# Turned-over attention rows kept in SBUF, attention operands on the other side of SBUF, token groups of 5, 6 and 5 blocks

## The chip, the cores and the metric

The kernel runs on one core of a Trainium2 chip. The metric is the device time of one launch in microseconds (us). The engines are PE (TensorE, matrix products), DVE (VectorE), ACT (ScalarE), POOL (GpSimd) and SP (SyncE, which here only issues transfers). Each engine executes its instructions in a fixed order; POOL and SP also issue DMA transfers, in that same order.

## The reference, cut to what matters

One layer of a hybrid decoder for a prompt of 2048 tokens and 8 single new tokens. A projection feeds two head groups: sparse attention (an indexer scores all earlier keys, the 256 best are kept, softmax over them) and a gated linear recurrence. Both outputs are joined, projected by `w_out` and added to x; a squared-ReLU MLP follows.

```python
h = rms_norm(x, norm1_g)
aq, ak, av, iq, ik, iw, rq, rf, ri, rg = jnp.split(h @ w_in, IN_OFFSETS, axis=-1)
...
att = attend(aq, ak, av, iq, ik, iw)             # top 256 keys by the indexer's scores, softmax over them
rec, S_new = hgrn2_mixer(rq, rf, ri, rg, lb, rec_norm_g, s0)
x = x + jnp.concatenate([att, rec.astype(att.dtype)], axis=-1) @ w_out
h2 = rms_norm(x, norm2_g)
x = x + jnp.square(jax.nn.relu(h2 @ w_up)) @ w_down
```

Widths: D = 1024, attention 512, recurrence 512, MLP 4096. The 8 new tokens attend to a paged cache of 16384 tokens each ("the sample"). All is float32.

## The kernel before, in words

The prompt is cut into 16 blocks of 128 tokens; block 16 stands for the 8 new tokens. Float32 accuracy is made of rounded parts: an operand is split into a high and a low part (`hh`/`hl`, `wh`/`wl`), and `mm3` (lines 126 to 129) runs three products.

`trunk` first does the projection, the recurrence and the indexer's scores for all blocks, and the choice of keys for blocks 2 to 7 (`early`, pool `px`). From about 1060 us on it goes through three groups of blocks, 0 to 5, 6 to 11 and 12 to 16:

- `attend` (function `attend_all`): for each block and each of 4 pairs of heads, logits `lg` against the keys `KS`, mask `MB` added on DVE, exponential on ACT, transposes `pt`, products with the values `VS` into `O`, back-transposes `ob`, and a scaling on POOL into the tile `att`. The finished `att` is stored to DRAM (`attD`, line 1028 and the lines after it). Keys, values and queries are loaded by DMAs on POOL's queue (`prep`, lines 939 to 960).
- `mlp` (function `mlp_group`): reads `attD` back as `mix` (`load_mix`), turns it over on PE (`transposed`, 4 transposes a block into `tp`) and splits it into `hh`, `hl`; projects by `w_out` (`po`, in four quarters `cq`); normalizes (`hn`, turned over into `hh`, `hl` again); then 16 panels of 256 hidden columns, each `up` (hidden values, in two token halves), ReLU and square on ACT (`rl`, `uh`), low part on DVE (`ul`, line 1705), and `dn` (products with `w_down`), which DVE adds to `y` (line 1729). Weights come in pieces of 512 KB: `raw` on SP's queue, a rounding copy on ACT (line 1550), and the low part from POOL (a subtraction at line 1554 in the first group, which stores it; from then on a DMA on POOL's queue at line 1552).

`recurrence_out` (recurrence rows times the lower half of `w_out`, `po<-wh,th`, kept in `yD`) is given to the scheduler beside the first group's attention. Two side tracks run along the first two MLPs: the choice of keys for blocks 8 to 11 and 12 to 15 (`Track` of `choose_all`, ACT and DVE), and the sample's parts (`part`): first the indexer's scores over the cache (indirect gathers `kg` on POOL, DVE transposes `kt`, splits `kh`, `kl`, products `sc`), then the search `tot`, a list of chosen rows, and 32 indirect gathers `KG`, `VG` on POOL (line 1473). A `Track` advances one step for every `rate` columns of matrix products (`PACE`, `PUMP`) that the MLP has put into the program; `issue_after` holds its instructions behind those last entered in the dictionary `front`.

The order on every engine is made at build time by a scheduler that simulates the program, with priorities (`high_priority`; a smaller one for stores, `LATE`). SBUF is given out by pools, from the left (low addresses) or the right; a tile in a place used before waits for the earlier tile's last use. Bytes of a partition: before, `p3` (with `hh`, `hl`, `y`) lies at 63424 to 152704, the attention's `pt` at 63424 upward and its `pk` with `KS`, `VS` at 123392 to 190976; `px` lies at 194528 to 224580.

Of the kernel before, what the change touches and what calls it, by code (L numbers as in the profile page):

```python
# [45 lines left out]
def hymba_kernel(ctx, tc, x_prompt, x_sample, cache_k, cache_v, cache_kidx, state_hgrn, page_table,  # L46
# [28 lines left out]
    def rows(t):  # L75
        return P if t < NB else NS
# [68 lines left out]
    GB = NB // NG  # L145


    GROUPS = range(6), range(6, 12), range(12, NB + 1)

    def trunk(ctx):  # L150

# [42 lines left out]
        def attend(tiles, LB, PT, OB):  # L194

            blocks = [b for b in tiles if b < NB]
            with tc.tile_pool(name="pt", bufs=1, reuse_waits="tile") as pt_, \
                 tc.tile_pool(name="pk", bufs=1, reuse_waits="tile") as pk, \
                 tc.tile_pool(name="qt", bufs=1, space=PSUM, reuse_waits="tile") as qt:
                yield from attend_all(pk, blocks)(pt_, qt, LB, PT, OB)  # L200

        def mlp(tiles):

            with tc.tile_pool(name="p3", bufs=1, reuse_waits="tile") as p3, \
                 tc.tile_pool(name="q3", bufs=1, space=PSUM, reuse_waits="tile") as q3:
                yield from mlp_group(tiles, p3, pw, q3, loads, E_IO, 2, 3, 4)
# [16 lines left out]
        choice = Track(choose_all(choose_block, range(AHEAD, GROUPS[2][0])), PACE[0])
        first = Track(part(), PUMP[0])
        with tc.tile_pool(name="pf", bufs=1, reuse_waits="tile") as pf, \
             tc.tile_pool(name="qf", bufs=1, space=PSUM, reuse_waits="tile") as qf:
            along(high(attend(GROUPS[0], 4, 2, 2), NEAR))
            recurrence_out(pf, qf)
        along(mlp(GROUPS[0]), choice, first)
        first.finish()  # L230
        choice.finish()
        choice = Track(choose_all(choose_block, GROUPS[2]), PACE[1])
        along(attend(GROUPS[1], 4, 4, 2))
        second = Track(part(), PUMP[1])
        along(mlp(GROUPS[1]), choice, second)
        second.finish()
        choice.finish()
# [661 lines left out]
    def recurrence_out(pf, qf):  # L899

        wh = pf.tile([P, 4, D], F32R, name="wh")
        wl = pf.tile([P, 4, D], F32R, name="wl")
        for k in range(4):
            raw = pf.tile([P, D], F32, tag="raw", name="raw", bufs=1)
            nc.sync.dma_start(raw, w_out[0, 512 + k * P:512 + (k + 1) * P])
            nc.scalar.copy(wh[:, k], raw)
            nc.gpsimd.tensor_tensor(wl[:, k], raw, wh[:, k].bitcast(F32), op=OP.subtract)
        for t in range(EARLY):
            rt = pf.tile([P, 512], F32, tag="rt", name="rt", bufs=2)
            nc.sync.dma_start(rt, recD[t * P:(t + 1) * P])  # L910
            y = pf.tile([P, D], F32, tag="y", name="y", bufs=2)
            nc.sync.dma_start(y, xp[t * P:(t + 1) * P])
            ps = qf.tile([P, 512], F32, tag="tp", name="tp", bufs=1)
            for k in range(4):
                nc.tensor.transpose(ps[:, k * P:(k + 1) * P], rt[:, k * P:(k + 1) * P], ident)
            th = pf.tile([P, 4, P], F32R, tag="th", name="th", bufs=2)
            tl = pf.tile([P, 4, P], F32R, tag="tl", name="tl", bufs=2)
            pv = ps.rearrange("p (k n) -> p k n", k=4)
            nc.scalar.copy(th, pv)
            nc.vector.tensor_tensor(tl, pv, th.bitcast(F32), op=OP.subtract)  # L920
            for hf in range(2):
                s = slice(hf * 512, (hf + 1) * 512)
                po = qf.tile([P, 512], F32, tag="po", name="po", bufs=1)
# [6 lines left out]
    def attend_all(pk, blocks):  # L930

        LEN = (blocks[-1] + 1) * P
        NC = (blocks[-1] + 4) // 4
# [98 lines left out]
        def attention(p2, q2, LB, PTB, OB):  # L1032
# [8 lines left out]
            for i, (b, u) in enumerate(units):  # L1041
# [542 lines left out]
    def w_out_parts(tiles):  # L1584
        return 1 if tiles[-1] < EARLY else 2

    def mlp_group(tiles, p3, pw, q3, loads, IO, MM, DN, UB):


        T = sum(rows(t) for t in tiles)  # L1590
# [5 lines left out]
        load_cols, load_row, load_mix = loads  # L1596

        def transposed(x, n, hi, lo, parts=2):

            for hf in range(parts):  # L1600
                ps = q3.tile([P, 512], F32, tag="dn", name="tp", bufs=DN)
                for k in range(4):
                    nc.tensor.transpose(ps[:, k * n:(k + 1) * n], x[:, (hf * 4 + k) * P:(hf * 4 + k + 1) * P], ident[:n, :n])
                pv = ps[:, :4 * n].rearrange("p (k n) -> p k n", k=4)
                hv = hi[:, hf * 4:hf * 4 + 4]
                nc.scalar.copy(hv, pv)
                nc.vector.tensor_tensor(lo[:, hf * 4:hf * 4 + 4], pv, hv.bitcast(F32), op=OP.subtract)

        hh = p3.tile([P, 8, T], F32R, tag="hh", name="hh")
        hl = p3.tile([P, 8, T], F32R, tag="hl", name="hl")  # L1610
# [162 lines left out]
```

## Time and profile before

| | us |
|---|---|
| median of 3 runs (3577.22 to 3578.02) | 3577.35 |
| the profiled execution | 3582.42 |
| its span, first to last instruction | 3580.7 |
| PE busy in the span | 3321.7 |
| DVE busy | 2341.7 |
| ACT busy | 2212.5 |
| mean granted PE clock, share of full speed | 0.965 |

The three groups lie so on the time axis: attention 0 from 1081 to 1291, MLP 0 to 1999, attention 1 from 2012, MLP 1 from about 2211 to 2903, attention 2 from 2912, MLP 2 from about 3122 to the end. In rows of waits, what stands behind "<-" is what was waited for.

### The profile page before, as it was taken

The page shows a single profiled execution, that of the slowest core. Times are in us where ns is not written, and L with a number is a line of the kernel's source. Part 1 is how long each engine was busy: PE and PEld are TensorE (multiplying, and loading weights), DVE is VectorE, ACT ScalarE, POOL GpSimd, SP SyncE. Part 2 cuts the span into 40 slices and gives each one's busy share as a digit, 9 for nine tenths or more (in the row PEclk, how much of TensorE's full clock was granted, in tenths as well). Part 3 has the DMA queues.
Part 4 walks back from the last instruction along what each step waited for, and adds up shares of the span by engine and source line. Part 5 has one row for each costly group of instructions (what it writes and reads, how often), then busy time and mean ns, then how long its engine had stood idle before and what let it go on. Part 6 is the DMA issues. An engine that isn't in the chain of part 4 may idle for free. (4 is left out here: it accounts for less than half of the span.)

```text
span 3580.7 us, 56788 instructions
## 1 busy us (share of the span) xinstructions
PE 3321.7 (93%) x20230; PEld 2911.3 (81%) x20230; DVE 2341.7 (65%) x5150; ACT 2212.5 (62%) x4063; POOL 1198.9 (33%) x1463
## 2 busy tenths in 40 slices
PE   8999989999998989999999898999699979889999
PEld 7786878999986778888888686889598868778888
DVE  3576798877773356898895588779636648633223
ACT  5789887767764347859843477476597337543332
POOL 5566676555552034544543110003400110021110
PEclk9999999999998999999999998899899989989999
DMA  7555556365534444555554411323443441155554
GB/s 213 161 171 162 155 162 181 112 165 142 156 109 164 137 163 145 186 164 155 168 190 141 156 46 50 113 95 107 144 127 109 153 163 36 42 186 168 177 169 143
DMA packets 347277, 509.13 MB, mean 142 GB/s; under 512 B 39048, under 2 KB 252016, under 8 KB 345840
## 3 DMA queue, kind: packets, MB, share of 16 engines
q1 hardware_dynamic: 284960, 333.96, 29.4%
q0 software_dynamic: 62032, 171.54, 15.9%
q8 instruction: 159, 2.61, 0.3%
q14 instruction: 126, 1.03, 0.1%
HBM read 379.25 MB, written 126.15 MB: 141 GB/s over the span
## 5 line engine op out<-in xcount | busy, mean ns | idle before, releaser
L509 ACT ACTIVATE jkA<-S,candA 128x1152 int8<-128x1152 f32 (+11 forms) x448 | 586.0, 1310 | 83.2 <-DVE candA L513 67.7
L1729 DVE TENSOR_TENSOR y<-y,dn 128x512 f32<-128x512 f32 x512 | 346.7, 682 | 304.6 <-PE dn L129 302.5
L127 PE MATMUL up<-hh,wh 128*128 128x384 f32 (+2 forms) x1536 | 493.3, 321 | 10.9 <-ACT wh L1550 5.7
L128 PE MATMUL up<-hl,wh 128*128 128x384 f32 (+2 forms) x1536 | 491.6, 320 | 0.0
L129 PE MATMUL up<-hh,wl 128*128 128x384 f32 (+2 forms) x1536 | 487.8, 321 | 3.1 <-DMA wl<-low 1.6
L128 PE MATMUL dn<-dl,uh 128*128 128x512 f32 x1024 | 405.8, 396 | 29.4 <-DMA dl<-low 29.4
L127 PE MATMUL dn<-dh,uh 128*128 128x512 f32 x1024 | 403.2, 397 | 2.1 <-DVE y L1729 1.5
L129 PE MATMUL dn<-dh,ul 128*128 128x512 f32 x1024 | 400.7, 394 | 0.0
L127 PEld LDWEIGHTS up<-hh,wh 128*128 128x128 f32 x1536 | 292.0, 190 | 22.9 <-ACT wh L1550 7.4
L128 PEld LDWEIGHTS up<-hl,wh 128*128 128x128 f32 x1536 | 292.2, 190 | 13.8 <-issue 4.2
L129 PEld LDWEIGHTS up<-hh,wl 128*128 128x128 f32 x1536 | 290.4, 190 | 12.5 <-POOL wl L1554 2.7
L1705 DVE TENSOR_TENSOR ul<-rl,uh 128x384 fp32r<-128x384 f32 (+1 forms) x192 | 117.2, 611 | 199.0 <-ACT uh L1704 197.7
L128 PEld LDWEIGHTS dn<-dl,uh 128*128 128x128 f32 x1024 | 193.5, 189 | 61.5 <-DMA dl<-low 30.2
L974 PE MATMUL lg<-KS,aqT 128*128 128x512 f32 (+3 forms) x640 | 199.8, 411 | 45.4 <-DMA KS<-ksD 34.2
L1550 ACT CAST dh<-raw 128x1024 fp32r<-128x1024 f32 x96 | 97.0, 1046 | 231.1 <-PE dn L129 223.3
L129 PEld LDWEIGHTS dn<-dh,ul 128*128 128x128 f32 x1024 | 193.2, 189 | 43.4
L983 ACT ACTIVATE L<-L,nm 128x128 f32<-128x128 f32 (+15 forms) x128 | 154.2, 1205 | 119.6 <-DVE nm L982 118.7
L127 PEld LDWEIGHTS dn<-dh,uh 128*128 128x128 f32 x1024 | 193.4, 189 | 39.6 <-DVE y L1729 3.8
L487 DVE SCALAR_TENSOR_TENSOR sl<-ix,iw,sl 128x512 f32<-128x512 f32 (+3 forms) x266 | 180.1, 677 | 59.1 <-ACT ix L483 56.6
L481 PE MATMUL ix<-IK,iqT 128*128 128x512 f32 (+3 forms) x608 | 187.9, 394 | 31.1 <-DVE sl L487 20.7
L483 ACT ACTIVATE ix<-ix,iw 128x512 f32<-128x512 f32 (+3 forms) x304 | 182.2, 603 | 50.8 <-PE ix L481 50.2
L1702 ACT ACTIVATE rl<-up 128x384 f32<-128x384 f32 (+1 forms) x192 | 86.8, 452 | 194.8 <-PE up L129 192.3
(497 smaller groups left out, 9270.5 us busy)
## 6 DMA issues: line engine op xcount, KB each, us to landing
raw<-in_w_up_dram SPq DMA_DIRECT2D x96, 512.0 KB
raw<-in_w_down_dram SPq DMA_DIRECT2D x96, 512.0 KB
wl<-low POOLq DMA_DIRECT2D x72, 512.0 KB
raw<-in_w_in_dram SPq DMA_DIRECT2D x256, 128.0 KB
dl<-low POOLq DMA_DIRECT2D x64, 512.0 KB
wl<-lowp POOLq DMA_DIRECT2D x48, 512.0 KB
low<-wl SPq DMA_DIRECT2D x40, 512.0 KB
low<-dl SPq DMA_DIRECT2D x32, 512.0 KB
```

The source lines that it names most:

```text
L127: nc.tensor.matmul(ps, lh, rh, start=first, stop=False)
L128: nc.tensor.matmul(ps, lh, rl, start=False, stop=False)
L129: nc.tensor.matmul(ps, ll, rh, start=False, stop=last)
L481: nc.tensor.matmul(ps[:, :kn], iqT[:, h], IK[:, i, k0:k0 + kn], start=i == 0, stop=i == 1)
L483: nc.scalar.activation(r[:, :kn], ps[:, :kn], AF.Relu, scale=iw[:, 1, h:h + 1])
L487: nc.vector.scalar_tensor_tensor(sl, r[:, :kn], iw[:, 2, h:h + 1], sl, op0=OP.mult, op1=OP.add)
L509: nc.scalar.activation(jk[:, :n], S[:, :n], AF.Sign, bias=cand.bitcast(F32), scale=-1.0, accum_out=cnt)
L974: nc.tensor.matmul(ps[:, :kn], aqT[:, 2 * u + j], KS[k0 // 512][:, u // 2, i, :kn], start=i == 0, stop=i == 1)
L983: nc.scalar.activation(L[:, :n], L[:, :n], AF.Exp, bias=nm, scale=ATT_SCALE, accum_out=sm[:, j:j + 1])
L1550: nc.scalar.copy(wh, raw)
L1705: nc.vector.tensor_tensor(ul[:, o], rl[:, :cn], uh[:, o].bitcast(F32), op=OP.subtract)
L1729: front["dve"] = nc.vector.tensor_tensor(ys_[t][:, s], ys_[t][:, s], po, op=OP.add)
```

## The change

1. **Turned-over rows.** A pool `ph` holds `hh` and `hl` of a group from before its attention until its MLP is done (`group_rows`). When a block's attention is finished, `turned` transposes `att` straight into it. `attD` and `mix` are used only for the 8 new tokens.
2. **Sides.** `pk` (keys, values, now also `aqT` and `MB`) is opened on the right side; `px` is closed before each attention and opened again after it (`choosing`). Bytes of a partition after: `ph` 63424 to 112576, `p3` and `pt` from 104384 (groups 0 and 2) or 112576 (group 1) upward, `pk` 163808 to 229344. `pk` then shares places with `px` and the sample's pools, and `pt` with `p3`'s `y`.
3. **Groups** of 5, 6 and 5 blocks (and the 8 new tokens). The choice still takes blocks 8 to 11 in MLP 0 and 12 to 15 in MLP 1.
4. **Smaller edits.** `front["pool"]` makes the tracks' instructions stand behind the last weight piece that POOL handled; `PUMP` 8000 becomes 7000 in MLP 0; `O` has one buffer in attention 0 (2 before), `L` 4 in attention 2 (5 before); `recurrence_out` has one `y` and two `po` buffers (2 and 1 before).

```diff
-    GROUPS = range(6), range(6, 12), range(12, NB + 1)
+    GROUPS = range(5), range(5, 11), range(11, NB + 1)
...
+        def group_rows(tiles):
+            T = sum(rows(t) for t in tiles)
+            ph = ctx_.enter_context(tc.tile_pool(name="ph", bufs=1, reuse_waits="tile"))
+            return [ph.tile([P, 8, T], F32R, name=x) for x in ("hh", "hl")]
...
-            with tc.tile_pool(name="pt", bufs=1, reuse_waits="tile") as pt_, \
-                 tc.tile_pool(name="pk", bufs=1, reuse_waits="tile") as pk, \
+            with tc.tile_pool(name="pk", bufs=1, side="right", reuse_waits="tile") as pk, \
+                 tc.tile_pool(name="pt", bufs=1, reuse_waits="tile") as pt_, \
...
+        with ExitStack() as ctx_:
+            rows_ = group_rows(GROUPS[1])
+            along(attend(GROUPS[1], rows_, 4, 4, 2))
+            choice = choosing(range(LATER, NB), PACE[1])
+            second = Track(part(), PUMP[1])
+            along(mlp(GROUPS[1], rows_), choice, second)
+            second.finish()
+            choice.finish()
+            cx.close()
...
-    PACE, PUMP = (12000, 14000), (8000, 9000)
+    PACE, PUMP = (12000, 14000), (7000, 9000)
...
-            aqT = p2.tile([P, NH, P], F32R, tag="aqT", name="aqT", bufs=2)
+            aqT = pk.tile([P, NH, P], F32R, tag="aqT", name="aqT", bufs=2)
...
                 if u == 3:
-                    (nc.gpsimd if b == blocks[-1] else nc.sync).dma_start(attD[b * P:(b + 1) * P], att)
+                    c = (b - blocks[0]) * P
+                    turned(q2, "pt", PTB, att, P, *(x[:, :, c:c + P] for x in rows_), 1)
...
-                nc.gpsimd.dma_start(wl, lowD[key])
+                front["pool"] = nc.gpsimd.dma_start(wl, lowD[key])
             else:
-                nc.gpsimd.tensor_tensor(wl, raw, wh.bitcast(F32), op=OP.subtract)
+                front["pool"] = nc.gpsimd.tensor_tensor(wl, raw, wh.bitcast(F32), op=OP.subtract)
...
-            if t < NB:
-                transposed(mx_[:n], n, hh[:, :, c:c + n], hl[:, :, c:c + n], 1 if t < EARLY else 2)
-            else:
-                transposed(mx_[:n], n, st[:, :, :NS], st[:, :, 32:])
+            if t == NB:
+                transposed(load_mix(t)[:n], n, st[:, :, :NS], st[:, :, 32:])
```

`turned` is the body of the former `transposed` with the PSUM pool and tag as arguments.

The instruction lists of PE, DVE and ACT hold the same operations with the same shapes in the same numbers before and after (the 64 block transposes read `att` instead of `mix`); what differs is their order, and that 16 stores to `attD` and 16 loads from it are gone. The order shows three places. The first is POOL in MLP 1, where the sample's row gathers `KG`, `VG` stand among the weight pieces `wl`, `dl` (`low`: a stored low part). Before:

```order
L1552 DMA wl<-low_19288 128x1024
L1552 DMA wl<-low_19296 128x1024
L1442 TENSOR_TENSOR ol<-o_28793,keyb 128x44x8
L1473 DMA KG<-in_cache_k_dram,idx 128x128 x16
L1473 DMA VG<-in_cache_v_dram,idx 128x128 x16
L1552 DMA dl<-low_19531 128x1024
L1552 DMA dl<-low_19539 128x1024
```

And now:

```order
L1572 DMA wl<-low_18649 128x1024
L1572 DMA wl<-low_18657 128x1024
L1462 TENSOR_TENSOR ol<-o_27908,keyb 128x44x8
L1493 DMA KG<-in_cache_k_dram,idx 128x128 x2
L1572 DMA dl<-low_18877 128x1024
L1572 DMA dl<-low_18885 128x1024
L1493 DMA KG<-in_cache_k_dram,idx 128x128 x4
L1572 DMA wl<-low_19055 128x1024
L1572 DMA wl<-low_19063 128x1024
L1493 DMA KG<-in_cache_k_dram,idx 128x128 x4
```

The next panel's `dl` stood behind all 32 gathers; it now stands behind two of them. The second place is POOL at the end of MLP 1, where the loads of attention 2 (`aqT`, `KS`, `VS`) stand. Before:

```order
L1552 DMA dl<-low_22892 128x1024
L1552 DMA dl<-low_22900 128x1024
L1552 DMA wl<-low_15776 128x1024
L1554 TENSOR_TENSOR wl<-raw,wh 128x1024
L1552 DMA wl<-low_15852 128x1024
L942 DMA aqT<-qsD 128x1024
L946 DMA KS_32390<-ksD 128x2048
L947 DMA VS_32394<-vsD 128x1024
```

And now:

```order
L1572 DMA wl<-low_21846 128x1024
L1572 DMA wl<-low_21854 128x1024
L961 DMA aqT<-qsD 128x1024
L965 DMA KS_31511<-ksD 128x2048
L966 DMA VS_31515<-vsD 128x1024
...
L966 DMA VS_31518<-vsD 128x1024
L1572 DMA dl<-low_21990 128x1024
L1572 DMA dl<-low_21998 128x1024
L1572 DMA wl<-low_22086 128x1024
L1572 DMA wl<-low_22094 128x1024
L1572 DMA dl<-low_22230 128x1024
L1572 DMA dl<-low_22238 128x1024
```

They stood behind the MLP's last weight piece (`low_22900`) and three pieces of the next `w_out`; they now stand ahead of the last two `dl` pairs and the last `wl` pair. DVE's last mask of the choice, which frees their place, stands ahead of the last 33 of the MLP's 192 additions to `y` (36 before). In the same way attention 1's loads now stand ahead of the last `dl` pair of MLP 0. The third place is PE between attention 2 and MLP 2. Before:

```order
L1013 MATMUL O<-pl,VS_32397 128x256
L1020 MATMUL ob<-ident,ot 128x128 x2
L1603 MATMUL tp<-ident,mix 128x128 x12
L127 MATMUL po<-wh,hh 128x256
L128 MATMUL po<-wl,hh 128x256
```

And now:

```order
L1032 MATMUL O<-pl,VS_31518 128x256
L1039 MATMUL ob<-ident,ot 128x128 x2
L1612 MATMUL tp<-ident,att 128x128 x4
L1612 MATMUL tp<-ident,mix 128x8 x8
L127 MATMUL po<-wh,hh 128x256
L128 MATMUL po<-wl,hh 128x256
L129 MATMUL po<-wh,hl 128x256
```

Only the last block's four transposes and the new tokens' eight are left between the attention and `w_out`; the others stand within the attention. At the start of attention 0 its first logits now stand among the last head's recurrence products (`lv`), and at its end the last three pairs of heads stand without products of `recurrence_out` between them.

## Rows read from the trace of the kernel before

**Rows 1.** The page's first part: engine, busy us, share of the span, instructions.

```profile
PE 3321.7 (93%) x20230; PEld 2911.3 (81%) x20230; DVE 2341.7 (65%) x5150; ACT 2212.5 (62%) x4063; POOL 1198.9 (33%) x1463
```

**Rows 2.** Busy time by stretch: length, engines, PE clock, DMA share, GB/s.

```profile
1060.00:1140.00 80.00, 62.47 (x277) 43.70 (x276) 26.98 (x109) 34.42 (x95) 32.99 (x40) 0.81 0.52 178
1280.00:1400.00 120.00, 95.96 (x589) 86.53 (x589) 68.01 (x154) 70.52 (x119) 47.17 (x52) 0.90 0.53 172
1400.00:1910.00 510.00, 491.79 (x2452) 436.06 (x2451) 448.53 (x863) 370.72 (x625) 238.98 (x162) 0.99 0.53 167
1995.00:2040.00 45.00, 29.47 (x148) 21.94 (x147) 22.63 (x68) 15.80 (x34) 7.63 (x15) 0.81 0.60 217
2195.00:2320.00 125.00, 101.63 (x639) 93.60 (x639) 97.08 (x232) 70.32 (x107) 11.70 (x25) 0.84 0.35 112
2540.00:2600.00 60.00, 26.78 (x125) 23.35 (x124) 26.90 (x75) 38.01 (x42) 30.13 (x30) 0.72 0.41 133
2895.00:2945.00 50.00, 29.89 (x144) 22.35 (x143) 22.39 (x63) 12.06 (x18) 6.71 (x13) 0.76 0.59 218
3100.00:3200.00 100.00, 80.84 (x569) 74.75 (x567) 38.34 (x70) 42.55 (x73) 20.14 (x32) 0.88 0.51 162
3200.00:3580.00 380.00, 376.16 (x2317) 326.48 (x2314) 114.61 (x190) 130.69 (x238) 41.19 (x118) 1.00 0.49 164
```

**Rows 3.** PE's waits, 2540 to 2600: who for whom, us, times, longest.

```profile
PE dn L128 <- DMA dl<-low: 28.3, 1, 28.3
```

**Rows 4.** POOL in order of time, 2480 to 2640: start, us, line, operation, idle before.

```profile
2529.68 1.10 POOL L1473 DMA_INDIRECT KG<-in_cache_k_dram,idx  x1 [20.05 <-DVE idx L1462]
...
2575.48 1.21 POOL L1552 DMA_DIRECT2D dl<-low  x2
...
2603.86 0.53 POOL L1552 DMA_DIRECT2D dl<-low  x1 [26.12 <-PE dn L129]
...
2636.29 0.53 POOL L1552 DMA_DIRECT2D dl<-low  x1 [20.21 <-PE dn L129]
```

**Rows 5.** PE's waits at the two switches from an MLP to an attention.

```profile
PE lg L974 <- DMA KS<-ksD: 15.0, 2, 12.5
PE lg L974 <- DMA KS<-ksD: 19.2, 4, 9.4
```

**Rows 6.** Chain that ended last, 2895 to 2945: start, us, what.

```profile
2907.01 18.50 DMA KS<-ksD
```

**Rows 7.** PE's waits from an attention to its MLP: 1280 to 1400, 2195 to 2320, 3100 to 3200.

```profile
PE po L127 <- ACT hh L1606: 6.7, 1, 6.7
PE tp L1603 <- DVE hn L1661: 5.3, 4, 2.2
...
PE tot L1317 <- DVE jk L1313: 8.3, 3, 5.1
...
PE tp L1603 <- DMA mix<-attD: 4.2, 2, 3.1
PE po L128 <- DMA wl<-low: 3.0, 1, 3.0
```

**Rows 8.** Two stretches of MLP 0, columns as in rows 2.

```profile
1560.00:1600.00 40.00, 33.68 (x164) 29.59 (x163) 38.43 (x66) 20.59 (x37) 17.06 (x10) 0.96 0.56 175
1800.00:1840.00 40.00, 35.84 (x171) 30.59 (x170) 39.87 (x61) 17.42 (x32) 19.61 (x15) 0.96 0.56 186
```

**Rows 9.** DVE's groups, 1400 to 1910: line, operation, count, busy us, mean ns.

```profile
L1729 DVE TENSOR_TENSOR y<-y,dn 128x512 f32<-128x512 f32 x150 | 99.7, 676 | 11.1 <-PE dn L129 10.6
L1705 DVE TENSOR_TENSOR ul<-rl,uh 128x384 fp32r<-128x384 f32 x50 | 39.1, 782 | 4.8 <-ACT uh L1704 3.7 <-ACT rl L1703 0.8
```

**Rows 10.** Waits of POOL and of PE, 1400 to 1910.

```profile
POOL kg L1249 <- DVE kt L1251: 176.6, 43, 13.5
...
PE up L129 <- POOL wl L1554: 0.8, 1, 0.8
```

**Rows 11.** DMA between 2895 and 2935: packets, bytes, mean rate.

```profile
DMA packets 2452, 10.88 MB, mean 272 GB/s; under 512 B 273, under 2 KB 273, under 8 KB 1938
```

More of the change, by code (lines that the diff above doesn't have):

```diff
@@ L192, in trunk, with attend, mlp @@
         loads = mlp_loads(pw, E_IO, E_WB)
[L194 removed]
+        def group_rows(tiles):
+            T = sum(rows(t) for t in tiles)
+            ph = ctx_.enter_context(tc.tile_pool(name="ph", bufs=1, reuse_waits="tile"))
+            return [ph.tile([P, 8, T], F32R, name=x) for x in ("hh", "hl")]
+        def attend(tiles, rows_, LB, PT, OB):
             blocks = [b for b in tiles if b < NB]
[L197 to L198 removed]
+            with tc.tile_pool(name="pk", bufs=1, side="right", reuse_waits="tile") as pk, \
+                 tc.tile_pool(name="pt", bufs=1, reuse_waits="tile") as pt_, \
                  tc.tile_pool(name="qt", bufs=1, space=PSUM, reuse_waits="tile") as qt:
[L200 to L202 removed]
+                yield from attend_all(pk, blocks, rows_)(pt_, qt, LB, PT, OB)
+        def mlp(tiles, rows_):
             with tc.tile_pool(name="p3", bufs=1, reuse_waits="tile") as p3, \
                  tc.tile_pool(name="q3", bufs=1, space=PSUM, reuse_waits="tile") as q3:
[L206 removed]
+                yield from mlp_group(tiles, p3, pw, q3, loads, rows_, E_IO, 2, 3, 4)
         def part():
@@ L221, in along, with choosing @@
                         t.step()
[L223 to L237, printed above, removed]
-        cx.close()
+        cx.close()
+        def choosing(blocks, rate):
+            px = cx.enter_context(tc.tile_pool(name="px", bufs=1, side="right", reuse_waits="tile"))
+            return Track(choose_all(choose_keys(px), blocks), rate)
+        with ExitStack() as ctx_:
+            rows_ = group_rows(GROUPS[0])
+            with tc.tile_pool(name="pf", bufs=1, reuse_waits="tile") as pf, \
+                 tc.tile_pool(name="qf", bufs=1, space=PSUM, reuse_waits="tile") as qf:
+                along(high(attend(GROUPS[0], rows_, 4, 2, 1), NEAR))
+                recurrence_out(pf, qf)
+            choice = choosing(range(AHEAD, LATER), PACE[0])
+            first = Track(part(), PUMP[0])
+            along(mlp(GROUPS[0], rows_), choice, first)
+            first.finish()
+            choice.finish()
+            cx.close()
+        with ExitStack() as ctx_:
+            rows_ = group_rows(GROUPS[1])
[4 more added lines that the diff above has]
+            second.finish()
+            choice.finish()
+            cx.close()
         for _ in picks:
             pass
-        along(attend(GROUPS[2], 5, 4, 2))
-        along(mlp(GROUPS[2]))
+        with ExitStack() as ctx_:
+            rows_ = group_rows(GROUPS[2])
+            along(attend(GROUPS[2], rows_, 4, 4, 2))
+            along(mlp(GROUPS[2], rows_))
     def high(steps, offset):
@@ L286, in choose_all @@
             yield "choice"
-    PACE, PUMP = (12000, 14000), (8000, 9000)
-    AHEAD = 8
+    PACE, PUMP = (12000, 14000), (7000, 9000)
+    LATER = 12
     NEAR = 100000
@@ L910, in recurrence_out @@
             nc.sync.dma_start(rt, recD[t * P:(t + 1) * P])
-            y = pf.tile([P, D], F32, tag="y", name="y", bufs=2)
+            y = pf.tile([P, D], F32, tag="y", name="y", bufs=1)
             nc.sync.dma_start(y, xp[t * P:(t + 1) * P])
@@ L922, in recurrence_out @@
                 s = slice(hf * 512, (hf + 1) * 512)
-                po = qf.tile([P, 512], F32, tag="po", name="po", bufs=1)
+                po = qf.tile([P, 512], F32, tag="po", name="po", bufs=2)
                 for k in range(4):
@@ L927, in recurrence_out, with attend_all @@
             store(yD[t], y)
-    def attend_all(pk, blocks):
+    def attend_all(pk, blocks, rows_):
         LEN = (blocks[-1] + 1) * P
@@ L952, in prep @@
             n = (b + 1) * P
-            MB = p2.tile([P, cols], BF, tag="MB", name="MB", bufs=2)
+            MB = pk.tile([P, cols], BF, tag="MB", name="MB", bufs=2)
             if n > TOPK:
@@ L1585, in w_out_parts, with turned, mlp_group @@
         return 1 if tiles[-1] < EARLY else 2
-    def mlp_group(tiles, p3, pw, q3, loads, IO, MM, DN, UB):
+    def turned(pool, tag, bufs, x, n, hi, lo, parts):
+        for hf in range(parts):
+            ps = pool.tile([P, 512], F32, tag=tag, name="tp", bufs=bufs)
+            for k in range(4):
+                nc.tensor.transpose(ps[:, k * n:(k + 1) * n], x[:, (hf * 4 + k) * P:(hf * 4 + k + 1) * P], ident[:n, :n])
+            pv = ps[:, :4 * n].rearrange("p (k n) -> p k n", k=4)
+            hv = hi[:, hf * 4:hf * 4 + 4]
+            nc.scalar.copy(hv, pv)
+            nc.vector.tensor_tensor(lo[:, hf * 4:hf * 4 + 4], pv, hv.bitcast(F32), op=OP.subtract)
+    def mlp_group(tiles, p3, pw, q3, loads, rows_, IO, MM, DN, UB):
         T = sum(rows(t) for t in tiles)
@@ L1598, in transposed @@
         def transposed(x, n, hi, lo, parts=2):
[L1600 to L1610, printed above, removed]
+            turned(q3, "dn", DN, x, n, hi, lo, parts)
+        hh, hl = rows_
         ys_ = {}
```

1 line of the change is left out of this document (removed).

## The prediction

> **What bounds the kernel now.** I read the page's first part, then the waits of PE, then busy time by stretch, then the order of time on POOL at the worst stretch. PE is busy 3321.7 of 3580.7 us, no other engine above 65% [rows 1], so PE is the bound as a whole and 259 us of PE idle time are all that a change of order can win, plus what the lower of the two clock levels (1.2 instead of 2.4 GHz) costs. The reader is to see in the stretches that the idle time isn't spread evenly: MLP 2 has 376 busy us in 380 at clock 1.00, MLP 0 492 in 510, but the seams between stages are poor, and each seam also shows a lower mean clock, 0.72 to 0.90 [rows 2]. The clock falls where PE stood idle before, and PE's next work then runs at the lower level.
>
> The instruction lists of PE, DVE and ACT are the same before and after, with the same shapes, so no term comes from more or less computing. Groups of 5, 6, 5 have token halves of 384 and 256, 384 and 384, 384 and 264 columns where 6, 6, 4 had twice 384 and 384, then 256 and 264: the same six. What a group loses another gains. The sum below is therefore one of idle time and clock, stretch by stretch. Idle is the stretch's length less PE's busy time; the clock costs at most (1 - clock) times busy, and less where the low clock fell into the idle time itself.
>
> **The change part by part.**
>
> *The gather stall (2540 to 2600).* Idle 33.2 us, clock at most 0.28 x 26.8 = 7.5 [rows 2]. PE waits once for 28.3 us for `dl` [rows 3]. On POOL the first gather waits 20 us for `idx`, 32 gathers follow until 2575.5, and only then comes `dl` [rows 4]. With two gathers ahead of it, `dl` would be issued about 2.5 us after 2529.7, or when its buffer is free, so before 2551, where PE began to wait. The rest of the gathers follow between later pieces. They finish some panels later (a panel of MLP 1 takes 2636.3 - 2603.9 = 32.4 us, rows 4), with their reader still panels away. I take 31; bounds 0 (the wait for `idx` still blocks the queue until too late) and 40.
>
> *From an MLP to the next attention (1995 to 2040, 2895 to 2945).* Idle 15.5 and 20.1, clock at most 5.6 and 7.2 [rows 2]; PE waits 15.0 and 19.2 for `KS` [rows 5], and in the chain of waits `KS` alone ends 18.5 us [rows 6]. The cause is the place: `KS` lay on `p3`'s uses, so loading began when the MLP ended. On the right side it waits for the choice and the sample, which end 33 additions, 33/12 = 2.75 panels or 89 us before MLP 1's end, and some 1.6 panels before MLP 0's. What is late next: `L` now lies on `y`, so the first logits wait for stores of `y`. In attention 2 the first `L` lies on `hl` and the first `y` tile, long free; in attention 1 on the third and fourth `y` of five, stored a few us behind the end. I take 11 and 20, bounds 5 to 18 and 12 to 25.
>
> *The loads' new place in POOL's queue.* They now stand ahead of the last two `dl` pairs. The attention's loads of some 7 MB moved at 272 GB/s as a mean [rows 11], so about 26 us. Of the 33 additions behind the choice 24 belong to the last two panels and 9 to the one before, so the loads are issued 9 additions of 1.35 us (16.2 us of `dn` over 12), 12 us, before that panel's end frees the next `dl` buffers; that `dl` is needed half a panel (16 us) later: 28 us against 26. I take a loss of 2, bounds 0 and 25. The Trainium skill speaks against this place: its page "DMA: Bandwidth & Descriptors", section "Queues, rings and completion order", says that a DMA engine consumes the descriptors of one ring in order, so weights issued behind the loads on one queue are served behind them. By that rule alone the `dl` pair comes after all 7 MB, which is the rival "loads ahead of weights" below; no row of before shows weights queued behind such loads.
>
> *From an attention to its MLP (1280 to 1400, 2195 to 2320, 3100 to 3200).* Idle 24.0, 23.4, 19.2; clock at most 9.6, 16.3, 9.7 [rows 2]. Store of `att`, load of `mix`, transposes and splits go from this seam: PE's waits that name them are 6.7 (for the split `hh`) and 4.2 (for `mix`); the waits of 8.3 for `tot` come from PE standing at the sample's first search product with little else to do ahead of it, and `w_out` now stands there [rows 7]. What stays: the normalization (`hn`, 5.3 in one seam, rows 7, with the clock behind it) and the last block's own chain `O`, `ot`, `ob`, `att`, now followed by four transposes on which PE has nothing to fill in: some 3 to 4 us a seam, as the copies on ACT, PE and POOL take about 0.4 us each in a row. Attention 0 ends with three pairs of heads without `recurrence_out` beside them; before, PE was 78% busy in the unfilled stretch from 1060 to 1140 [rows 2], and three pairs of about 4 us at that rate lose 3, with one `O` buffer perhaps 5. I take 8, 16 and 11; bounds 0 to 25, 8 to 25, 5 to 18.
>
> *From the recurrence to attention 0 (1060 to 1140).* Idle 17.5, clock at most 11.9 [rows 2]. The recurrence's last head and the short first blocks were each too thin to fill PE; they now interleave, since `pk` and `pt` lie where the indexer and the early choice are done. I take 12, bounds 0 and 22.
>
> *MLP 0 gets denser.* It keeps the same choice and nearly the same sample work, in panels of 5/6 the size: 27 instead of 32.4 us of PE. DVE was busy 448.5 of 510 us [rows 2], 88%. Of that 99.7 are additions to `y` and 39.1 low parts [rows 9], so 310 are side work, over 12.5 panels 24.8 each. The sample now ends at 14 panels of 16 (13 before), so 23 a panel, with 9.4 of the MLP's own (10 additions, 4 low parts of 5/6 length), 32.4 together against a panel of 27 + 8 of the sample's own products = 35: 93%. Where DVE was busy 96 to 100%, PE lost 6.3 and 4.2 us in 40 [rows 8]. Five per cent more work makes about three more such stretches; I take a loss of 15. Bounds 0 and 75 (as thin as 1280 to 1400, 80% busy, over 470 us, less the 18 idle there now).
>
> *At nothing.* The stores and loads of `attD` besides (8 MB in all), `L` with 4 buffers and the transposes' use of the `pt` banks inside the attentions: hidden by the next pair's logits. They cost at most a few us a block where that cover is missing; I take a loss of 2.
>
> **Sum.** 31 + 11 + 20 + 8 + 16 + 11 + 12 = 109, less 2, 15 and 2: 90. The profiled execution took 3582.4 us and would take 3492; the median of the runs shown lies 5 lower, so 3577 - 90 = 3487 us.
>
> **Rivals.**
>
> - *Loads ahead of weights.* `dl` queues behind the attention's loads at both switches, and the PE stall of the seam is only moved into the MLP. Then 11 + 20 are not won and some 10 more may go on the low clock: 3487 + 31 + 10 = 3528. For it: the rows of the order, and 28 against 26 is a thin margin. Against: MLP 0's last `dl` is computed on POOL, not loaded, and the rate of 272 is a mean that holds idle time too.
> - *The gather stall stays*, as `idx` comes later than the buffer is free and the queue stands still before the first gather: 3487 + 31 = 3518. For it: 20 of the stall's 46 us on POOL are that wait [rows 4]. Against: PE wasn't yet waiting when `idx` came.
> - *Slower: POOL's queue binds MLP 0.* POOL's gathers `kg` waited 43 times for DVE's `kt`, 176.6 us, longest 13.5 [rows 10]; behind them stand the subtractions that make `wl` and `dl`, now in panels that are 5.4 us shorter. If each of 14 panels made PE wait for one such subtraction, the cost is 14 x 4.1 (the mean) = 57 or 14 x 13.5 = 189 us in place of the 15. It decides against the change from (90 + 15) / 14 = 7.5 us a panel; at 9 the time is 3487 - 15 + 126 = 3598. For it: POOL is busy 239 of 510 us and waits for most of the rest. Against: a gather waits because it runs ahead of its buffers, which costs nobody unless a piece stands behind it at that moment, and PE waited 0.8 us for `wl` there [rows 10].
> - *The change doesn't do what it says*: the tiles of `pk` wait for something on the right side that ends with the MLP (a late mask store), and only the turned rows help: 3487 + 31 = 3518, as the first rival without its clock.
>
> **How the numbers follow.** The forecast gets 0.64, with its own range of 3455 to 3520; the three partial ones together 0.24 (3515 to 3550, both stalls staying 3560); the slower one 0.08; a result at the old time, gains and MLP 0's loss cancelling, 0.04. About 0.2% (7 us) is what a measurement of this kernel can tell from no change. So faster 0.88, same 0.04, slower 0.08. If all seams give their upper bounds and MLP 0 loses nothing, 109 becomes about 170 less 2, but not together; I set the low end at 3440. The high end is 3560, and a tenth or so is left outside.
>
> **What would show it.** In the changed profile: the PE wait for `dl` in MLP 1 gone and the gathers spread over several panels; `KS` no longer among PE's longest waits at the starts of attentions 1 and 2, its issue some 90 us ahead of MLP 1's end; no `tp<-mix` of 128 columns; the stretches at the seams with a mean clock above 0.9; MLP 0's PE share slightly lower than 492/510 and DVE's above 90%. PE's busy time should change little apart from the low clock, whose share (mean 0.965) should rise to about 0.98. The forecast is wrong if MLP 0's panels take over 40 us with PE waiting for POOL, or if new waits for `dl` stand near the end of MLP 1.

## The result

The changed kernel takes 3516.17 us as a median of 4 runs, the kernel before 3577.68 us beside it: a ratio of 0.9829, 95% interval [0.9812, 0.9846]. It is faster by 61.5 us; 90 were forecast. The time lies in the range of 3440 to 3560, but by itself it says little: 3516 lies in the forecast's own 3455 to 3520 and also in the 3515 to 3550 of the partial rivals. The stages tell more. The gather stall and the switches to an attention moved about as argued; MLP 0 lost nearly three times what was forecast; and attention 0 won 16 us more than forecast, which made up for over half of that miss. That part is luck.

To see where the time went, each trace is cut at the same events (end of the indexer; first `up` and last `dn` of each MLP), and each stage gets one number: PE's idle time plus half of its busy time at 1.2 GHz. What is left of the time is PE's work as it would be at full clock: 3246 us before and 3250 after, so the loss is what changed. The gains add up to 70 us; less the 3.4 of work, that is what lies between the two profiled executions (3582.42 and 3515.95):

| stage | before | after | forecast gain | gain |
|---|---|---|---|---|
| up to the indexer's end | 84.0 | 84.6 | 0 | -1 |
| A0: attention 0 with its seams | 58.7 | 22.4 | 12 + 8 | 36 |
| M0: MLP 0 | 26.2 | 68.9 | -15 | -43 |
| A1: attention 1 with its seams | 56.3 | 37.4 | 11 + 16 | 19 |
| M1: MLP 1 | 46.5 | 17.8 | 31 - 2 | 29 |
| A2: attention 2 with its seams | 55.7 | 27.4 | 20 + 11 | 28 |
| M2: MLP 2 | 2.6 | 1.7 | 0 | 1 |

The "at nothing" loss of 2 has no row of its own.

### The profile page after: what moved, and what is told of

The parts are those of the page before. It is cut to its first block, busy times and chain, and to the rows that moved or that the text cites. A ratio compares the mean times of both kernels' runs of the same rounds, so it can differ in the third digit from the quotient of the medians.

```text
span 3514.2 us, 56706 instructions
## 1 busy us (share of the span) xinstructions
PE 3315.7 (94%) x20230; PEld 2912.1 (83%) x20230; DVE 2345.8 (67%) x5150; ACT 2202.5 (63%) x4063; POOL 1201.2 (34%) x1460
## 5 line engine op out<-in xcount | busy, mean ns | idle before, releaser
L528 ACT ACTIVATE jkA<-S,candA 128x1664 int8<-128x1664 f32 (+11 forms) x448 | 586.3, 1310 | 116.8 <-DVE candA L532 101.4
L127 PEld LDWEIGHTS up<-hh,wh 128*128 128x128 f32 x1536 | 294.9, 192 | 18.2 <-ACT wh L1570 4.9
L1724 DVE TENSOR_TENSOR ul<-rl,uh 128x384 fp32r<-128x384 f32 x192 | 114.3, 597 | 157.2 <-ACT uh L1723 155.9
L1572 POOL DMA_DIRECT2D dl<-low x64 | 34.9, 545 | 521.9 <-PE dn L129 477.9
L1269 POOL DMA_INDIRECT kg<-in_cache_kidx_dram,pti x128 | 132.3, 1033 | 210.7 <-DVE kt L1271 180.1
```

The costliest lines, as they stand in the source:

```text
L127: nc.tensor.matmul(ps, lh, rh, start=first, stop=False)
L528: nc.scalar.activation(jk[:, :n], S[:, :n], AF.Sign, bias=cand.bitcast(F32), scale=-1.0, accum_out=cnt)
L1269: nc.gpsimd.indirect_dma_start(out=kg_, out_offset=None, in_=kview, in_offset=bass.IndirectOffsetOnAxis(ap=pti[:, b, g, u:u + 1], axis=0))
L1724: nc.vector.tensor_tensor(ul[:, o], rl[:, :cn], uh[:, o].bitcast(F32), op=OP.subtract)
```

## The profile after

The page's first line, against [rows 1]:

```profile
PE 3315.7 (94%) x20230; PEld 2912.1 (83%) x20230; DVE 2345.8 (67%) x5150; ACT 2202.5 (63%) x4063; POOL 1201.2 (34%) x1460
```

PE's mean clock rose from 0.965 to 0.977. The stretches of the changed kernel that answer to [rows 2], with the same columns:

```profile
1056.00:1136.00 80.00, 71.47 (x402) 53.41 (x401) 36.38 (x124) 42.02 (x108) 39.39 (x38) 1.00 0.60 197
1220.00:1320.00 100.00, 89.05 (x537) 74.81 (x536) 49.86 (x137) 51.77 (x98) 29.34 (x41) 0.91 0.40 132
1330.00:1860.00 530.00, 486.33 (x2543) 428.30 (x2542) 474.41 (x882) 386.23 (x669) 259.40 (x170) 0.95 0.55 174
1890.00:1935.00 45.00, 40.22 (x219) 30.90 (x217) 30.85 (x93) 24.69 (x51) 5.05 (x11) 0.96 0.31 105
2065.00:2185.00 120.00, 100.59 (x649) 92.55 (x649) 99.94 (x245) 70.04 (x108) 13.54 (x28) 0.90 0.32 108
2390.00:2450.00 60.00, 54.50 (x273) 48.88 (x272) 39.44 (x88) 32.78 (x44) 22.16 (x26) 0.99 0.58 200
2730.00:2780.00 50.00, 44.76 (x246) 35.18 (x245) 36.30 (x94) 27.32 (x43) 5.22 (x7) 0.93 0.29 98
2945.00:3045.00 100.00, 88.28 (x646) 81.99 (x645) 49.02 (x98) 45.44 (x78) 17.17 (x31) 0.93 0.37 122
```

All got better (the recurrence's end from clock 0.81 to 1.00, the gathers' stretch from 33.2 us idle in 60 to 5.5) but the third: MLP 0 now idles 43.7 us in 530, where it idled 18.2 in 510, at clock 0.95 in place of 0.99, with DVE 90% busy.

PE's waits of 1890 to 1940, then of 2600 to 2760, which answer to [rows 5]:

```profile
PE lg L993 <- DVE mx L995: 3.9, 5, 2.4
...
PE pt L1016 <- ACT L L1002: 3.4, 1, 3.4
PE dn L128 <- DMA dl<-low: 1.3, 1, 1.3
```

`KS` is gone from them. POOL in order of time around the gathers, against [rows 4]:

```profile
2389.72 1.09 POOL L1493 DMA_INDIRECT KG<-in_cache_k_dram,idx  x1 [20.21 <-DVE idx L1482]
2391.11 0.98 POOL L1493 DMA_INDIRECT KG<-in_cache_k_dram,idx  x1 [0.31 <-issue]
2395.16 1.25 POOL L1572 DMA_DIRECT2D dl<-low  x2 [3.08 <-PE dn L129]
```

Two gathers, then `dl`, 5 us after the first gather instead of 46. The 20 us that the queue stands for `idx` stayed and cost PE nothing. In MLP 0 PE's longest waits are:

```profile
PE sc L1230 <- DVE kl L1283: 11.1, 4, 4.4
PE sc L1230 <- DVE rs L1238: 10.1, 4, 4.0
PE dn L129 <- DVE ul L1724: 5.0, 2, 3.1
PE sc L1230 <- DVE need L566: 4.4, 1, 4.4
PE dn L128 <- POOL dl L1574: 3.4, 2, 2.1
```

The four longest are for DVE; POOL's piece has the shortest of these five.

## Experiments

Each starts from the changed kernel and changes only what is named. Loss by stage in us as above (the changed kernel: 85, 22, 69, 37, 18, 27, 2 in the table's order):

| run | median us | ratio to before | pre | A0 | M0 | A1 | M1 | A2 |
|---|---|---|---|---|---|---|---|---|
| groups 6, 6, 4 | 3516.1 | 0.982 | 87 | 46 | 38 | 44 | 20 | 26 |
| no POOL front | 3560.3 | 0.995 | 90 | 31 | 75 | 40 | 46 | 27 |
| blocks 8, 9 chosen early | 3523.6 | 0.985 | 116 | 22 | 38 | 41 | 18 | 29 |
| att through DRAM | 3540.8 | 0.989 | 87 | 34 | 72 | 41 | 14 | 29 |
| half of kl on POOL | 3536.0 | 0.989 | 86 | 22 | 83 | 42 | 20 | 28 |
| block 11 chosen later | 3549.6 | 0.993 | 83 | 23 | 49 | 38 | 19 | 80 |
| sample slower | 3515.9 | 0.984 | 87 | 21 | 50 | 52 | 19 | 28 |
| block 8 chosen early | 3521.5 | 0.985 | 106 | 21 | 58 | 35 | 14 | 27 |
| three lanes | 3494.7 | 0.977 | 83 | 22 | 48 | 33 | 22 | 28 |
| three lanes, sample slower | 3499.6 | 0.978 | 84 | 22 | 39 | 51 | 20 | 27 |
| the changed kernel again | 3516.2 | 0.984 | 87 | 22 | 70 | 39 | 15 | 27 |
| low parts zero | 3480.7 | 0.972 | 87 | 28 | 15 | 54 | 16 | 28 |

**Groups 6, 6, 4.** `GROUPS = range(6), range(6, 12), range(12, NB + 1)`, and in group 0 `LB` 3, `ph` and `pl` with 2 buffers.

> The groups part alone is undone (6, 6, 4 again; the turned rows' own pool, the other side for the attention's operands and the block-by-block filling stay; group 0 has a buffer less for L, ph and pl, so that it fits). Idle time and low clock inside MLP 0 cost 26 us before and 69 us in the changed kernel. Theory A (the same choice and sample on DVE in a shorter MLP 0 are what costs the 43 us): MLP 0 loses 25 to 40 us again and the time is 3485 to 3500 us. Theory B (the front that ties POOL's gathers to the pieces costs it) and C (the pace of the sample's steps): it stays near 65 to 80 us and the time is 3510 to 3530 us.

MLP 0 got 31 us back, as theory A said, but the time didn't move (3485 to 3500 were expected): A0 lost 23 more and A1 7. The first load of attention 0's `KS` on POOL (start, us), in this run, then in the changed kernel:

```profile
1067.14 0.55 POOL L965 DMA_DIRECT2D KS<-ksD  x1
```

```profile
610.59 0.54 POOL L965 DMA_DIRECT2D KS<-ksD  x1
```

With five blocks it is issued 445 us ahead of the indexer's end, with six 10 us behind it, as in the kernel before (1067.0). So the new groups as such are worth nothing here: A0 and A1 win what MLP 0 loses. Of A0's 23, 14 lie up to 1145 us, at the recurrence's end, and 7 at the seam to the MLP (from 1275 us); the block more and the three buffers less of group 0 aren't separated from the late `KS`.

**No POOL front.** `front["pool"] = ` is dropped from both lines of `parts`.

> Only the line that records POOL's last subtraction as the front of the gathers goes, so that the gathers may be issued in one row again. Theory A: MLP 0 keeps its loss of 69 us within 8, and in MLP 1 PE waits for dl once for 25 to 35 us again: 3540 to 3552 us. Theory B: MLP 0's loss falls to some 30 us, which pays for the stall: 3500 to 3515 us.

The wait is back at 30.4 us (PE's waits, 2370 to 2480), M1 loses 28 more, MLP 0 doesn't improve, and the time lies above the expected 3540 to 3552:

```profile
PE dn L128 <- DMA dl<-low: 31.6, 2, 30.4
```

This shows the gather term, and that the ties don't cause MLP 0's loss. Its profiled run loses 52 us more in all: the stall's 28, 9 in A0, 6 in MLP 0, 5 in the stage ahead. Why those others move wasn't looked into.

**Blocks 8 and 9, or 8 alone, chosen early.** `AHEAD = 10`, `AHEAD = 9`.

> The choice of blocks 8 and 9 is moved from MLP 0 to the stage ahead of attention 0; MLP 0 keeps blocks 10 and 11 and the sample. Theory A: DVE's share in MLP 0 falls from about 95 to about 80 per cent and MLP 0 loses 25 to 35 us in place of 69; the stage ahead gets longer by 0 to 40 us, so 3480 to 3520 us as a whole. Theories B and C: MLP 0's loss stays above 55 us.

> The choice of block 8 alone is moved ahead of attention 0 (with blocks 8 and 9 the stage ahead lost 31 us more and MLP 0 31 us less). If both go by the block, MLP 0 loses 50 to 56 us and the stage ahead 98 to 102: 3512 to 3522 us. Rival: the two lanes of the early choice have room for one block beside the scores of the last ones; then the stage ahead loses under 92 us and the time is 3498 to 3508 us.

MLP 0's loss falls to 38 and 58, both just above what was expected, but the stage ahead loses 31 and 22 more. By their medians the two runs are 7 and 5 us slower than the changed kernel, the second within the spread of its own executions (3511 to 3526). The work costs at least as much there; the room for one block, the second run's rival, isn't there.

**att through DRAM.** The `turned(...)` call in the attention becomes the old store to `attD`, and `load_mix` with its transposes returns.

> The turned rows of att are undone: att is stored to DRAM and loaded as mix, transposed and split behind the attention, as before; everything else of the change stays. Forecast of the first document's steps: the three seams from an attention to its MLP, which now lose 12, 25 and 15 us, go back towards 27, 34 and 27: 3540 to 3555 us. Rival: the seams won by the buffers' new side and w_out's new place alone, and the turned rows are worth nothing: 3510 to 3520 us. MLP 0's loss stays within 10 us of 69 by theory A.

25 us slower: 12 in A0, 3 in A1 and 1 in A2 by idle time and clock, 8 as full-clock work of PE that these three stages have more (why, no row shows). So the turned rows pay, but less at the seams of attentions 1 and 2 than forecast.

**Half of kl on POOL.** `(nc.gpsimd if e else nc.vector).tensor_tensor(kl, ...)`.

> Sixty of the 120 low parts kl of the sample's first search are computed on POOL in place of DVE; all else as in the changed kernel. That takes some 60 us of DVE's busy time out of MLP 0 and puts 60 subtractions of 1.2 to 1.8 us on POOL, which holds the gathers and the MLP's own subtractions. Theory A (DVE's side work is too dense for the shorter MLP 0): its loss falls from 69 to 35 to 50 us, 3482 to 3500 us as a whole. Rival: DVE is only one of several limits, or POOL's queue takes its place: MLP 0 loses 65 us or more, 3512 to 3560 us.

Theory A failed here: 60 operations fewer on DVE, and MLP 0 lost 14 us more. DVE's groups of MLP 0 show why, and POOL's behind them (busy us, mean ns):

```profile
L1283 DVE TENSOR_TENSOR kl<-kt,kh 128x512 fp32r<-128x512 f32 x60 | 69.5, 1166 | 4.3 <-ACT kh L1282 1.9 <-issue 1.4 <-ACT rl L1722 0.8
...
L532 DVE SCALAR_TENSOR_TENSOR candA<-incA,candA 128x1 int32<-128x1 int32 x114 | 52.1, 462 | 2.1
...
L1283 POOL TENSOR_TENSOR kl<-kt,kh 128x512 fp32r<-128x512 f32 x60 | 82.7, 1379 | 52.9 <-ACT kh L1282 24.7 <-DVE ul L1724 9.3 <-ACT SC L1248 6.0
```

What stayed on DVE took longer each time. This led to theory D, below.

**Block 11 chosen later.** `LATER = 11`.

> The choice of block 11 moves from MLP 0 to MLP 1, by one number. In MLP 1 the last mask then stands behind the last addition, so the operands of attention 2 can only be issued when MLP 1 has ended, as before the change. Theory A for MLP 0: its loss falls from 69 to 50 to 58 us. The step on the operands' place: PE waits 14 to 20 us for KS at attention 2 again, and the stretch from MLP 1 to MLP 2 loses 42 to 48 us in place of 27. As a whole 3512 to 3525 us. Rival to that step: the seam was won by something else (the clock, the stores of y); then KS stays under 5 us among PE's waits and the time is 3500 to 3508 us.

MLP 0's loss, 49, is just below the expected 50 to 58. A2 is far off: 80 for 42 to 48, and the time with it (3512 to 3525 expected). PE waits for `KS` (2720 to 2960), and POOL's issue shows the cause:

```profile
PE lg L993 <- DMA KS<-ksD: 52.6, 2, 49.7
```

```profile
2761.53 0.54 POOL L965 DMA_DIRECT2D KS<-ksD  x1
```

MLP 1 ended at 2718; the last search ran on alone to 2742 and its masks to 2760. I had priced the load and not the search in front of it.

**Sample slower.** `PUMP = (8000, 9000)`.

> The sample's steps in MLP 0 get 8000 columns each in place of 7000, by one number: they end at 157 of 160 additions (140 now), so that the operands of attention 1 are issued behind MLP 0's weights and near its end. The operands' place: PE waits 8 to 15 us for KS at attention 1 (none now) and the stretch from MLP 0 to MLP 1 loses 45 to 52 us in place of 37. Theory A for MLP 0: the same DVE work spread over 12 per cent more of the stage, so its loss falls to 50 to 62 us. As a whole 3508 to 3522 us. Theory C (the pace alone is what costs): MLP 0's loss falls below 45 us.

Both halves came true: MLP 0 19 us better, A1 14 worse, with PE waiting for `KS` (1880 to 1945):

```profile
PE lg L993 <- DMA KS<-ksD: 11.5, 2, 8.4
```

This is the price of the operands' early place at that seam (11 forecast).

**Three lanes.** `LATER = 11`, `choose_all(..., lanes)` with 3 lanes in MLP 1 and an own `S` of 14 x 128 columns for the third; in the second run also `PUMP = (7500, 9000)`. **The changed kernel again** ran beside them.

> The choice of block 11 moves to MLP 1 as in the run before of that kind, but MLP 1 now chooses three blocks beside each other in place of two (a third buffer for S of 14 x 128 columns), so that its last mask stands at addition 161 of 192 (159 in the changed kernel, 192 in that run), ahead of the MLP's last weights. Theory A with the operands' place: MLP 0 loses 49 us in place of 69, MLP 1 18 to 28 in place of 18 (its DVE is busy 392 of 580 us), and KS doesn't return among PE's waits at attention 2, so the stretch behind MLP 1 keeps its 27: 3494 to 3506 us. Rival (a third lane makes DVE in MLP 1 as dense as in MLP 0): MLP 1 loses over 40 us, 3516 us or more.

> As the run with three lanes, and the sample's steps in MLP 0 get 7500 columns in place of 7000 (the run with 8000 took 19 us off MLP 0 and put 14 on the seam behind it). The sample ends at addition 146 of 160, still some 19 us of additions ahead of the end, less than the 50 us that PE waited for KS where it was issued at the end of MLP 1. Theory A: MLP 0 loses 38 to 45 us, the seam to MLP 1 37 to 43 in place of 37: 3486 to 3502 us. Rival: the seam takes what MLP 0 gives, within 4 us of the run with three lanes.

> The changed kernel once more, beside the two runs with three lanes, so that they are compared on one chip: 3514 to 3518 us, MLP 0 losing 66 to 72 us.

Three lanes beat both kernels: 0.9773 [0.9757, 0.9790] of before, and 3493.6 to 3499.3 us where the changed kernel took 3515.2 to 3524.5 on the same chip. MLP 1, whose DVE has room, takes the work for 4 us where MLP 0 paid 21 (7 and 22 against the changed kernel's second run). The slower sample beside it won 9 more in MLP 0 and lost 17 at the seam, though not to `KS`: the seam took more than MLP 0 gave, against the forecast for it, and the run is 5 us slower than three lanes alone. There DVE waits for the store of `y` (1850 to 1920):

```profile
DVE L L995 <- DMA out_dram<-y: 14.2, 1, 14.2
```

This is what the prediction called late next in attention 1 (`L` lies on `y`), with a larger price. It stands in the two runs in which MLP 0 ended earliest, this one (1863 us) and the next (1845), and not with three lanes alone (1872); why the store was late wasn't looked into.

**Low parts zero.** In `parts`, `for part in (wl, wl, wl[:, :shape[1] // 2]): front["pool"] = nc.gpsimd.memset(part.bitcast(F32), 0.0)` replaces the subtraction.

> In MLP 0 and its w_out POOL doesn't compute the weights' low parts (left out: they are zeros, so their products add nothing); in place of each subtraction of 2.5 us it fills the tile by two and a half memsets of about 1 us, so that POOL is about as busy but doesn't read SBUF. Products, additions, choice and sample are all still there. In the changed kernel 16 of the 120 kl in MLP 0 ran at the same time as such a subtraction and took 3.47 us as a mean, the other 104 took 0.69; the additions y, with an operand in PSUM, took 0.68 us either way. Theory D (DVE stands still while POOL's subtraction runs, and that is the part of MLP 0's DVE time that the forecast left out): the mean of kl falls from 1.06 to 0.70 us, DVE's busy time in the 520 us from 1340 on from 466 to 380 to 410, MLP 0 loses 25 to 42 us in place of 69, and the time is 3470 to 3492 us. Rival 1 (any work of POOL does it, or they only come at the same moments): kl stays at 0.95 us or more and MLP 0's loss within 8 us of 69. Rival 2 (DVE gets shorter, but PE waits for the chain of the sample's steps, not for DVE's time): kl falls to 0.70 and MLP 0 still loses 55 us or more, 3502 us or more.

Theory D holds. DVE's groups of MLP 0, first of before, then of the changed kernel, then of this run (count | busy us, mean ns):

```profile
L1263 DVE TENSOR_TENSOR kl<-kt,kh 128x512 fp32r<-128x512 f32 x120 | 112.5, 958 | 12.4 <-ACT kh L1262 11.6 <-ACT rl L1703 0.6
L513 DVE SCALAR_TENSOR_TENSOR candA<-incA,candA 128x1 int32<-128x1 int32 x112 | 24.3, 226 | 2.0
```

```profile
L1283 DVE TENSOR_TENSOR kl<-kt,kh 128x512 fp32r<-128x512 f32 x120 | 124.2, 1057 | 13.7 <-ACT kh L1282 10.4 <-ACT rl L1721 1.9 <-PE sc L1230 0.7
L1748 DVE TENSOR_TENSOR y<-y,dn 128x512 f32<-128x512 f32 x160 | 107.2, 679 | 29.7 <-PE dn L129 28.0 <-issue 0.8 <-PE dn L128 0.2
L1724 DVE TENSOR_TENSOR ul<-rl,uh 128x384 fp32r<-128x384 f32 (+1 forms) x64 | 46.5, 729 | 10.3 <-ACT uh L1723 10.2
L1240 DVE SCALAR_TENSOR_TENSOR rw<-rs,rw 64x512 fp32r<-64x512 f32 x31 | 32.9, 1060 | 3.7 <-ACT rw L1239 2.9
L532 DVE SCALAR_TENSOR_TENSOR candA<-incA,candA 128x1 int32<-128x1 int32 x114 | 28.6, 258 | 1.9
```

```profile
L1749 DVE TENSOR_TENSOR y<-y,dn 128x512 f32<-128x512 f32 x160 | 107.6, 680 | 43.6 <-PE dn L129 43.1
L1283 DVE TENSOR_TENSOR kl<-kt,kh 128x512 fp32r<-128x512 f32 x120 | 79.3, 685 | 17.7 <-ACT kh L1282 16.4 <-PE sc L1230 1.3
L1725 DVE TENSOR_TENSOR ul<-rl,uh 128x384 fp32r<-128x384 f32 (+1 forms) x64 | 30.9, 483 | 14.5 <-ACT uh L1724 14.1
L1240 DVE SCALAR_TENSOR_TENSOR rw<-rs,rw 64x512 fp32r<-64x512 f32 x31 | 21.2, 685 | 9.5 <-ACT rw L1239 8.8
L532 DVE SCALAR_TENSOR_TENSOR candA<-incA,candA 128x1 int32<-128x1 int32 x114 | 16.8, 154 | 1.8
```

`kl`, `ul`, `rw` and `candA` became shorter by 84 us in all with the same shapes and counts; `y` stayed at 0.68. POOL was as busy as before (260.3 us from 1340 to 1860, 259.2 in the changed kernel), and 24 of the `kl` ran beside a memset and took 0.68 us, so for these four it isn't POOL's activity as such. PE's waits for `kl`, `rs` and `ul` are gone (11.1, 10.1 and 5.0 in the changed kernel), and MLP 0 loses 15 in place of 69, better than the 25 to 42 expected. Two other differences of this run don't explain that: a memset needn't wait for the rounding copy, but PE's waits for POOL's pieces were 4.5 us in all; and MLPs 1 and 2 load the same stored zeros and lose 16 and 3, where the changed kernel loses 18 and 2. Of the 54 won, 17 went to A1, where DVE waits 16.8 us for the store of `y` again, and 5 to A0.

## Why the prediction came out as it did

**The step that failed: "MLP 0 gets denser", 15 for 43.** DVE's share wasn't set too low: 93% of a panel were forecast, and DVE is busy 90% of the time from 1330 to 1860. What failed is the step from that share to PE's loss, "about three more such stretches". The working took DVE's busy time before as work of fixed length. But that busy time held stalls: by the mean durations of the last run, shape by shape, and the counts above, 84 us of the changed kernel's 499 us of DVE in MLP 0 are `kl`, `ul`, `rw` and `candA` standing still beside POOL's subtractions. An operation of 0.7 us then takes up to 7, PE's products `sc` and `dn` wait behind it, and then the clock falls (of the 43, 26 are idle time and 17 the lower clock). So not three stretches thinned but the whole stage.

The stalls themselves weren't new. Before, the same four groups lost some 67 us to them (33, 18, 8 and 8), while PE lost 26 in MLP 0; `kl` and `candA` are shown above, the other two here (count | busy us, mean ns):

```profile
L1705 DVE TENSOR_TENSOR ul<-rl,uh 128x384 fp32r<-128x384 f32 x64 | 53.5, 837 | 34.0 <-ACT uh L1704 32.9 <-ACT rl L1703 0.8
L1220 DVE SCALAR_TENSOR_TENSOR rw<-rs,rw 64x512 fp32r<-64x512 f32 x31 | 29.5, 951 | 9.0 <-ACT rw L1219 8.3
```

The 64 subtractions and nearly the same side work now fall into 592 us in place of 633. How much of the 43 comes from the 17 us of stalls more, and how much from the old ones with less of PE's work around them, stays open: the kernel before wasn't run without them. What is shown is that either remedy works. With the stalls gone (low parts zero) or less side work a panel (blocks chosen elsewhere, a slower sample, longer panels) the loss goes down each time; three lanes keep some 86 us of stalls and still lose 21 less. With more subtractions on POOL it goes up.

**A0, 36 for 20.** By the same count the recurrence's end (to about 1145 us) lost 31 before and loses 9 now, and the seam to the MLP (from 1283 and from 1244 us) 27 and 12: 22 and 15 where I had taken 12 and 8, the first at its upper bound of 22. The runs that undo a part show some of it. Without the turned rows A0 loses 12 more, 11 of them at the seam. In the run with six blocks, where `KS` comes late, 14 of the 22 at the recurrence's end are gone: attention 0 can't fill the recurrence's last head there. The rest isn't separated.

**A1 and A2, 19 for 27 and 28 for 31.** The places of `KS` gave about what was forecast: in some 46 us behind the MLP's end the switch from MLP 0 lost 18 before and 6 now, the one from MLP 1 25 and 8, so 12 for 11 and 16 for 20. The seam to MLP 1 gave about half of its 16: of the wait for `tot` (8.3 before) 4.9 us remained, one of 5.3 for `y` of `w_out` (L1698) came, and `hn` stayed as expected (5.4) [rows 7]:

```profile
PE tp L1612 <- DVE hn L1680: 5.4, 4, 3.0
PE po L127 <- DVE y L1698: 5.3, 2, 4.6
PE tot L1337 <- DVE jk L1333: 4.9, 1, 4.9
```

A2's other 12 lie at its seam to MLP 2 (27 before, 15 now, 11 forecast). The turned rows gave back only 3 and 1 us of idle time and clock at these two seams when they were undone; what else won there isn't separated.

**M1, 29 for 29.** Shown by undoing it: 28 are lost again.

**The rivals.** *Loads ahead of weights*: refuted as a cost. The loads were issued from 2656.3 to 2671.2 and the next `dl` at 2675.7, and from 2656 to MLP 1's end PE waits for no weight at all; the 1.3 us for `dl` shown above stand at 2617, ahead of the loads. The ring order cited from the Trainium skill's "DMA: Bandwidth & Descriptors", section "Queues, rings and completion order", isn't refuted by that: DMA moved 391 GB/s from 2657 to 2690, above the 272 of [rows 11], so the weights could come in time even in order. *The gather stall stays*: refuted by the order of time on POOL. *POOL's queue binds MLP 0*: PE waited 4.5 us for POOL's `dl` and `wl` there, so not through its queue; yet POOL did bind it, through DVE. I had named the right engine with the wrong mechanism. *The change doesn't do what it says*: refuted by `KS`, issued from 2656.8 on, 79 us ahead of MLP 1's end.

## What to carry to other kernels

Before adding up an engine's busy time, compare one operation's mean with its shortest: here a spread from 0.7 to 7 us for one shape was a stall counted as work, and a shorter stage didn't shrink it (67 us before, 84 after). Side work belongs where its engine has room (DVE 392 of 580 us in MLP 1, 90% in MLP 0), provided that its last step still ends ahead of the loads that lie on its buffers. A seam that is freed shows the next wait in line: in two runs here the store of `y` under `L`.

## What the hardware showed

In these runs a DVE operation with two operands in SBUF stands still until POOL's subtraction is over, and the profile counts the wait as DVE's busy time. In MLP 0 of the changed kernel the 16 `kl` that ran beside such a subtraction took 3.47 us as a mean (two of them 0.68, the others 1.5 to 7.2), the other 104 at most 0.74. The longest, on DVE and then on POOL (start, us):

```profile
1764.01 0.68 DVE L1748 TENSOR_TENSOR y<-y,dn 128x512 f32<-128x512 f32 x1
1764.60 0.14 DVE L559 TENSOR_SCALAR ge<-ngt 128x1 f32<-128x1 f32 x1
1764.67 7.21 DVE L1283 TENSOR_TENSOR kl<-kt,kh 128x512 fp32r<-128x512 f32 x1
...
1764.20 4.78 POOL L1574 TENSOR_TENSOR dl<-raw,dh 128x1024 fp32r<-128x1024 f32 x2
1768.93 2.38 POOL L1574 TENSOR_TENSOR wl<-raw,wh 128x1024 fp32r<-128x1024 f32 x1
```

`kl` came 0.5 us behind the first of three subtractions and ended 0.57 us behind the last, about its own length. `y`, with one operand in PSUM, took 0.68 us either way. The Trainium skill says this in "SBUF — State Buffer", section "SBUF: two separate sides": the port pair that the two engines share is locked for a whole instruction and the loser blocks, for a DVE operation with two SBUF inputs only against a GpSimd operation that reads SBUF. The traces agree in both parts: 7.21 us behind three subtractions, and 0.68 for the 24 `kl` beside memsets.

Memsets aren't harmless to every DVE operation. In the run with low parts zero two of the five `tb` of this shape, with one tensor operand in SBUF, took 5.7 us beside a row of memsets and a third 1.2; the other two took 0.62. The first, on DVE and then on POOL (start, us):

```profile
1493.51 5.71 DVE L552 TENSOR_SCALAR tb<-S,candA 128x768 bf16<-128x768 f32 x1
1494.21 4.59 POOL L1575 MEMSET wl<- 128x1024 f32 x6
```
